# Compression pre-activations kept in PSUM, and softmax scales, minima and sums without two-tensor SBUF operations on VectorE

## The chip, the cores and the metric

The kernel runs on one core of a Trainium2 chip (trn2). The metric is the device time of one execution in microseconds (us); several runs are taken and their median is given. A profile of one execution gives, for every instruction of TensorE (PE, its weight loads PEld), VectorE (DVE), ScalarE (ACT), GpSimd (POOL) and of the DMA queues, when it started and how long it took.

## The reference, cut to what matters

One step of a decoder trunk: a prompt of 1024 tokens and eight single tokens, each with 8192 cached positions. The parts that the change touches are the compression of keys and values into blocks and the three softmax branches of the attention over the prompt:

```python
def compress(k, pe, w1, w2):                     # k: (B, T, G, 64)
    ...
    hid = pe.reshape(-1) @ w1                    # a bias
    for j in range(CMP_SEGS):                    # 2 segments of 16 positions
        hid = hid + jnp.einsum('bnsgd,sdh->bngh', seg[:, j:j + nc], w1r[j])
    return jax.nn.silu(hid) @ w2

def nsa_attend(...):
    s_c = jnp.einsum('bqgrd,bcgd->bgrqc', q, kc) + bias_c
    p_c = jax.nn.softmax(jnp.where(valid_c, s_c, NEG), axis=-1) * valid_c
    ...                                          # the same for selected blocks (p_s) and the window (p_w)
    g = jax.nn.sigmoid(gates)
    o = g[..., 0:1] * o_c + g[..., 1:2] * o_s + g[..., 2:3] * o_w
```

`compress` runs over the prompt's new rows and over the 8 x 8192 cached rows of keys and of values. All data are float32.

## The kernel before, in words

The program has three stages. The first (to about 440 us) projects the prompt and does the retention heads. The middle stage weaves two streams together: `attention()` over the prompt, and `compression()` of the caches with the decode attention behind it. The last stage does the output projection, the feed-forward network and the gated embedding.

`weave` takes generators that yield estimated costs and always advances the one with the smallest sum. It fixes the order in which instructions are issued, and a tile layer moves them a little against each other on each engine's queue. Every engine then works through its own queue in order and waits on semaphores.

**Attention** goes over 32 units (a 128-row tile of queries, a key group, a pair of heads; class `Unit`). Each has three branches: compressed (0), selected (1), window (2). For a branch, TensorE makes negated scores in PSUM banks `s`. VectorE adds the bias there and takes the minimum, `nmx`; where the scores have two pieces, the minimum of the second comes into a one-element tile `m2` and is joined to the first (L1080, helper line L139). ACT makes the exponentials into `pcm`, `psel` or `pwin` in SBUF with their sums in `sm` (L1094). Two partial sums are added (L1097, helper line L148). Then `scale` takes the reciprocal (L1046), multiplies it by the gate `gsig` (L1047, helper line L145) and multiplies the branch's tile by the product `scl`: on POOL for branches 0 and 2 (L1056), on ACT for branch 1 (L1052), as `ON = "GAG"` says. Last, `values` transposes the tiles on TensorE (L1141), ACT copies and rounds them (`ph`, L1146), VectorE takes the rest (`pl`, L142), and TensorE multiplies with the values (L1130, L1132).

**Compression** goes over 32 blocks (16 of keys, then 16 of values; a block is half of one sequence's cache). POOL gathers its pages by indirect DMA (L939), VectorE transposes them into `seg` tiles (L947), and the difference of two of them is taken half on VectorE and half on POOL (`differ`, L142). TensorE runs three passes of 8 matmuls (each stands twice in the trace, L918) into a PSUM bank `m`, of which there are two: with the weights of the second segment, then, on the block before, with the difference of the weights (`w1l` in the rows), then with those of the first segment. The hidden values are gated by silu as (tanh(x/2) + 1) * x/2:

```python
V.scalar_tensor_tensor(x, ph[:, :256], w[3][:, 0:1], d..., op0=ALU.add, op1=ALU.add)   # L1000
A.activation(t, x, AF.Tanh, scale=0.5)                                                # L1002
gated(pd, t, x, xhid[n][:, :, 128:256])                                               # L820
```

That is one half of a block's columns. The other half follows a block later in `hidden_act` (L826, L828), after the second pass has added to the same columns of the bank. In both, `x` (tile `ch_x`) and `t` (tile `ch_t`) are in SBUF, and `gated` (L820) makes the product `xh` from them on VectorE. A bank goes to the block after next once all that read it are done. `bank(...)` tiles are in PSUM, `tl(...)` tiles in SBUF. `prompt_blocks` uses `hidden_act` twice for the prompt's own rows.

Helpers record under one line whoever calls them: L139 any operation, L142 subtract, L145 multiply, L148 add.

Of the kernel before, what the change touches and what calls it, by code (L numbers as in the profile page):

```python
# [14 lines left out]
AF = mybir.ActivationFunctionType  # L15
ALU = mybir.AluOpType
AX = mybir.AxisListType.X
# [19 lines left out]
W_ATT, W_ATT2, W_DEC, W_VAL, W_RET, W_SP, W_T, ON, ORD = 1.6, 1.8, 0.5, 1.0, 3.0, (9000.0, 0.0, 6000.0, 0.0), (4000.0, 9000.0), "GAG", (0,7,1,6,2,5,3,4)  # L37
# [83 lines left out]
def hybrid_kernel(tc, I, C, O):  # L121
    nc = tc.nc
    V, G, A, P, SY = nc.vector, nc.gpsimd, nc.scalar, nc.tensor, nc.sync
# [6 lines left out]
    def tl(pool, shape, tag, dt=F32, bufs=None):  # L130
        kw = {} if bufs is None else {"bufs": bufs}
        return pool.tile(shape, dt, tag=tag, name=nm(tag), **kw)
# [5 lines left out]
    def tt(eng, out, a, b, op):  # L138
        eng.tensor_tensor(out=out, in0=a, in1=b, op=op)  # L139
# [4 lines left out]
    def mul(eng, out, a, b):  # L144
        eng.tensor_tensor(out=out, in0=a, in1=b, op=ALU.mult)  # L145

    def add(eng, out, a, b):
        eng.tensor_tensor(out=out, in0=a, in1=b, op=ALU.add)  # L148
# [34 lines left out]
    gsig = tl(pcd, [128, 9, 24], "gsig")  # L183
# [490 lines left out]
    for pair in range(2):  # L674
        rqk = tl(pr, [128, 2, 2, T], "rqk", bufs=1)
        rgs = tl(pr, [128, 2, T], "rgs", bufs=1)
        if pair:
# [3 lines left out]
            for t in range(9):  # L681
                pt, r = tok_major(wts, 256, t)
# [136 lines left out]
    def gated(p, t, x, dst):  # L819
        V.scalar_tensor_tensor(dst, t.rearrange("p (g n) -> p g n", g=2), 1.0, x.rearrange("p (g n) -> p g n", g=2),  # L820
                               op0=ALU.add, op1=ALU.mult)

    def hidden_act(p, w, ph, n, dst):

        t = tl(p, [128, 2 * n], "ch_t", bufs=2)
        A.activation(t[:, :2 * n], ph[:, :2 * n], AF.Tanh, bias=w[3][:, 1:2], scale=0.5)  # L826
        x = tl(p, [128, 2 * n], "ch_x", bufs=2)
        A.activation(x[:, :2 * n], ph[:, :2 * n], AF.Identity, bias=w[3][:, 0:1])  # L828
        gated(p, t[:, :2 * n], x[:, :2 * n], dst)


    def prompt_blocks():
# [121 lines left out]
    def compress_halves(n0, n1, w, tail, lag):  # L954

        done = n0
        phs, odd = {}, {}

        def parts(n, which):
            return seg[n, which, 0], seg[n, which, 1]  # L960

        for n in range(n0, n1 + 1):
            if n < n1:
                _, b, h = HALVES[n]
                ph = phs[n] = bank("m", 2)
                for k, _ in enumerate(half_mm(ph, w[1], parts(n, 0), True)):
                    if k in (0, 3):
                        turn_segments(n, 1, k // 3)
                    if k in (2, 5):
                        differ(n, k // 5)  # L970
                    if k in (6, 7):
                        fetch(n + 1, 1, [2 * k - 12, 2 * k - 11])
                    yield 430.0

                a = firsts[n] = tl(pd, [128, 2, 129], "first", bufs=2)
                A.copy(a[:, :, 0:128], ph[:, :256].rearrange("p (g n) -> p g n", g=2))
                if h:
                    G.memset(a[:, :, 128:129], 0.0)
                else:
                    G.tensor_copy(a[:, :, 128:129], firsts[n - 1][:, :, 0:1])  # L980
                d = tl(pd, [128, 2, 128], "follow", bufs=2)
                sub(G, d, a[:, :, 1:129], a[:, :, 0:128])
            if n > n0:
                m = n - 1
                for _ in half_mm(phs[m], w[4], parts(m, 2), False):
                    yield 430.0
                hidden_act(pd, w, phs[m], 128, xhid[m][:, :, 0:128])
            if n < n1:
                for k, _ in enumerate(half_mm(ph, w[0], parts(n, 1), False)):
                    if k in (0, 3):  # L990
                        turn_segments(n + 1, 0, k // 3)
                    if k in (5, 6):
                        fetch(n + 2, 0, [2 * k - 10, 2 * k - 9])
                    if k == 3 and done <= n - (1 if "ready" in E else lag):
                        yield from tail(done)
                        done += 1
                    yield 430.0
                xhid[n] = tl(pd, [128, 2, 256], "xh", bufs=4)
                x = tl(pd, [128, 256], "ch_x", bufs=2)
                V.scalar_tensor_tensor(x, ph[:, :256], w[3][:, 0:1], d.rearrange("p g n -> p (g n)"), op0=ALU.add, op1=ALU.add)  # L1000
                t = tl(pd, [128, 256], "ch_t", bufs=2)
                A.activation(t, x, AF.Tanh, scale=0.5)  # L1002
                gated(pd, t, x, xhid[n][:, :, 128:256])
                if "ready" in E and done <= n - 2:
                    yield from tail(done)
                    done += 1
        yield 1500.0
        for n in range(done, n1):
            yield from tail(n)
# [19 lines left out]
    class Unit:  # L1029
# [14 lines left out]
        def scale(u, br, dst, width, nmx, sm):  # L1044
            scl = tl(pp, [128, 2], "scl", bufs=4)
            V.reciprocal(scl, sm)  # L1046
            mul(V, scl, scl, gsig[:, u.i, br * 8 + u.h0:br * 8 + u.h0 + 2])  # L1047
            if u.i == 0 and br == 0:
                mul(V, scl, scl, rowv.to_broadcast([128, 2]))
            for r in range(2):  # L1050
                if ON[br] == "A":
                    A.mul(dst[:, r, :width], dst[:, r, :width], scl[:, r:r + 1])  # L1052
                elif ON[br] == "V":
                    V.tensor_scalar(dst[:, r, :width], dst[:, r, :width], scl[:, r:r + 1], None, op0=ALU.mult)
                else:
                    G.tensor_scalar(dst[:, r, :width], dst[:, r, :width], scl[:, r:r + 1], 1.0, op0=ALU.mult, op1=ALU.mult)  # L1056

        def branch(u, br, pieces, kind, dst, base_):
            nmx = tl(pp, [128, 2], "nmx", bufs=4)
            sm = tl(pp, [128, 2, 2], "sm", bufs=4)  # L1060
            for r in range(2):
                banks = []
                for x, (k0, n) in enumerate(pieces):
# [12 lines left out]
                    if lo < hi:  # L1076
                        if got:
                            m2 = tl(pp, [128, 1], "m2", bufs=4)
                            V.tensor_reduce(out=m2, in_=b[:, lo:hi], op=ALU.min, axis=AX)
                            tt(V, mn, mn, m2, ALU.min)  # L1080
                        else:
                            V.tensor_reduce(out=mn, in_=b[:, lo:hi], op=ALU.min, axis=AX)
                        got = True
# [9 lines left out]
                for x, (k0, n) in enumerate(pieces):  # L1093
                    A.activation(dst[:, r, (k0 - base_) * 128:(k0 - base_ + n) * 128], banks[x][:, :n * 128], AF.Exp,  # L1094
                                 bias=nmx[:, r:r + 1], scale=-1.0, accum_out=sm[:, r, x:x + 1])
            if len(pieces) == 2:
                add(V, sm[:, :, 0], sm[:, :, 0], sm[:, :, 1])  # L1097
            u.scale(br, dst, pieces[-1][0] * 128 + pieces[-1][1] * 128 - base_ * 128, nmx, sm[:, :, 0])

        def near_scores(u):  # L1100
            wc, nc0 = u.wc, max(0, u.wc - 15)
# [982 lines left out]
```

## Time and profile before

| | |
|---|---|
| median of 3 runs | 2201.52 us (2194.11 to 2202.75) |
| the profiled execution | 2201.91 us, its span 2200.1 us |
| mean granted TensorE clock | 0.977 of full speed |
| busy: PE, PEld | 2074.9 us (94%), 1912.1 us (87%) |
| busy: DVE, ACT, POOL | 1420.3 us (65%), 834.0 us (38%), 677.9 us (31%) |

The span runs from the first to the last instruction of the profiled execution. Matmuls are pipelined and the ends of their bars are modelled, so a busy PE is not a PE at its peak. A row of a group gives its busy time, the mean of one instruction, and the idle time of the engine just before them with what ended it. A row of a timeline gives start and duration; what stands in brackets is the idle time of the engine before it and its releaser.

### The profile page before, as it was taken

Reading aid. Unit: us, or ns where it says so; the run is one execution under the profiler, and the core shown is the slowest. Engines: PE = TensorE matmul, PEld = TensorE weight load, DVE = VectorE, ACT = ScalarE, POOL = GpSimd, SP = SyncE. Lnnn points to the kernel's source line nnn. Section 1 sums busy time; section 2 is a strip of 40 time slices with the busy share of each in tenths; the row PEclk is TensorE's granted clock in tenths of the full one; section 3 lists DMA queues with packets and bytes.
Section 4 is the critical chain, followed back from the end, with each engine's and each line's share of the span. In section 5 each row is a group of like instructions: output and inputs, shape, how many; then the busy total and the mean of one; then the engine's idle time right before and its main releaser. Section 6 shows DMA issues by size and latency. Waiting matters only on the chain. (4 is left out here: it accounts for less than half of the span.)

```text
span 2200.1 us, 38626 instructions
## 1 busy us (share of the span) xinstructions
PE 2074.9 (94%) x14856; PEld 1912.1 (87%) x14856; DVE 1420.3 (65%) x3231; ACT 834.0 (38%) x2027; POOL 677.9 (31%) x891
## 2 busy tenths in 40 slices
PE   7999999979899898899999899999999999999998
PEld 6998998867677776667999899999999999999998
DVE  4335245357788888768677437866766677878632
ACT  3331222235454454444444433332332334533321
POOL 1234334276666665656665023000000000000100
PEclk9999999979999999999999999999999999999999
DMA  6312213244333334443553442223223325644321
GB/s 220 126 58 70 68 51 83 61 131 122 100 107 106 96 106 123 151 147 119 164 156 114 125 148 78 73 92 112 97 92 109 103 92 176 193 118 144 92 78 49
DMA packets 183696, 244.65 MB, mean 111 GB/s; under 512 B 16980, under 2 KB 152808, under 8 KB 183320
## 3 DMA queue, kind: packets, MB, share of 16 engines
q1 hardware_dynamic: 158424, 158.28, 23.5%
q0 software_dynamic: 25088, 83.90, 12.4%
q8 instruction: 117, 1.92, 0.4%
q14 instruction: 67, 0.55, 0.1%
HBM read 201.99 MB, written 44.32 MB: 112 GB/s over the span
## 5 line engine op out<-in xcount | busy, mean ns | idle before, releaser
L918 PE MATMUL m<-seg,w1h 128*128 128x256 f32 x1024 | 302.9, 402 | 0.6 <-issue 0.6
L157 PE MATMUL s<-x,wu 128*128 128x258 f32 x872 | 249.4, 286 | 4.0 <-ACT x L152 1.4
L158 PE MATMUL s<-x,wu 128*128 128x258 f32 x872 | 248.6, 285 | 0.7 <-DVE x L142 0.7
L159 PE MATMUL s<-x,wu 128*128 128x258 f32 x872 | 247.9, 284 | 0.5 <-DVE wu L142 0.5
L157 PE MATMUL m<-x,wu 128*128 128x258 f32 x768 | 219.9, 287 | 3.7 <-DVE h L148 1.7
L158 PE MATMUL m<-x,wu 128*128 128x258 f32 x768 | 218.5, 285 | 2.5 <-DVE x L142 2.5
L159 PE MATMUL m<-x,wu 128*128 128x258 f32 x768 | 218.5, 285 | 0.0
L142 POOL TENSOR_TENSOR x<-h,x 128x516 fp32r<-128x516 f32 x4 | 5.6, 1412 | 677.4 <-ACT x L152 677.4
L918 PEld LDWEIGHTS m<-seg,w1h 128*128 128x128 f32 x1024 | 176.0, 197 | 19.8 <-issue 8.8
L947 DVE STREAM_TRANSPOSE seg<-raw 128x1024 f32<-128x1024 f32 x128 | 158.4, 1238 | 37.9 <-PE m L918 21.5
L152 ACT CAST wu<-wu 128x512 fp32r<-128x512 f32 (+2 forms) x178 | 109.6, 626 | 190.7 <-DVE wu L142 115.6
L157 PEld LDWEIGHTS s<-x,wu 128*128 128x128 f32 x872 | 166.0, 191 | 5.2 <-ACT x L152 1.9
L158 PEld LDWEIGHTS s<-x,wu 128*128 128x128 f32 x872 | 166.7, 191 | 1.3 <-DVE x L142 1.2
L159 PEld LDWEIGHTS s<-x,wu 128*128 128x128 f32 x872 | 166.4, 191 | 0.7 <-DVE wu L142 0.7
L142 DVE TENSOR_TENSOR wu<-wu,wu 128x512 fp32r<-128x512 f32 (+2 forms) x178 | 125.3, 707 | 59.6 <-ACT wu L152 57.9
L157 PE MATMUL t<-x,wu 128*128 128x258 f32 x528 | 151.2, 286 | 4.8 <-DVE h L148 1.9
L285 PE MATMUL g<-wh,xnh 128*128 128x256 f32 (+3 forms) x504 | 149.8, 298 | 2.3 <-ACT xnh L335 2.1
L157 PEld LDWEIGHTS m<-x,wu 128*128 128x128 f32 x768 | 146.6, 191 | 5.7 <-issue 1.7
L158 PE MATMUL t<-x,wu 128*128 128x258 f32 x528 | 150.0, 284 | 0.9 <-DVE x L142 0.9
L159 PE MATMUL t<-x,wu 128*128 128x258 f32 x528 | 149.7, 284 | 0.3 <-DVE wu L142 0.3
L158 PEld LDWEIGHTS m<-x,wu 128*128 128x128 f32 x768 | 147.1, 192 | 2.7 <-DVE x L142 2.7
L159 PEld LDWEIGHTS m<-x,wu 128*128 128x128 f32 x768 | 146.7, 191 | 0.0
(476 smaller groups left out, 6028.9 us busy)
## 6 DMA issues: line engine op xcount, KB each, us to landing
act_d<-act SPq DMA_DIRECT2D x22, 903.0 KB
wr<-in_w_in_dram SPq DMA_DIRECT2D x12, 1024.0 KB
wu<-in_w_gate_dram SPq DMA_DIRECT2D x22, 512.0 KB
wu<-in_w_up_dram SPq DMA_DIRECT2D x22, 512.0 KB
st<-act_d SPq DMA_DIRECT2D x42, 258.0 KB
wu<-in_w_down_dram SPq DMA_DIRECT2D x16, 512.0 KB
wst<-act_d SPq DMA_DIRECT2D x28, 258.0 KB
mr<-mix_d SPq DMA_DIRECT2D x16, 258.0 KB
```

What stands on the lines that cost most here:

```text
L142: eng.tensor_tensor(out=out, in0=a, in1=b, op=ALU.subtract)
L152: A.copy(hi, src)
L157: P.matmul(out, wh, xh, start=first, stop=False, **kw)
L158: P.matmul(out, wh, xl, start=False, stop=False, **kw)
L159: P.matmul(out, wl, xh, start=False, stop=last, **kw)
L285: P.matmul(pt[:r, :n], xh, wh[:, k, :n], start=k == 0, stop=False)
L918: P.matmul(out, w[:, k, :], x[:, k // 2 % 2, :, k % 2, :], start=first and k == 0, stop=k == 7, skip_group_check=not first)
L947: V.transpose(t.rearrange("p k (x d) -> p k x d", x=4), raws[n, par][:, :, s2 * 256:(s2 + 1) * 256].rearrange("p x (k d) -> p k x d", k=8))
```

## The change

Five edits, all around softmax and gating:

1. `hidden_act`: `x` is no longer a tile in SBUF but the bank's own columns; the Identity with the bias writes them in place.
2. `compress_halves`: `x` is the upper half of the bank (`ph[:, 256:512]`); the sum is written there and Tanh and `gated` read it there.
3. `scale`: the reciprocal is no longer multiplied by the gate on VectorE. POOL takes both factors as per-partition scalars of one instruction; for branch 1, ACT multiplies the reciprocal by the gate first, one column at a time.
4. `branch`, minima: the join of two minima takes one tensor and a per-partition scalar in place of two tensors.
5. `branch`, sums: a reduction over the pair in place of an addition of its two halves, into a tile of its own.

```diff
--- before.py
+++ after.py
@@ -823,10 +823,10 @@
     def hidden_act(p, w, ph, n, dst):
 
         t = tl(p, [128, 2 * n], "ch_t", bufs=2)
-        A.activation(t[:, :2 * n], ph[:, :2 * n], AF.Tanh, bias=w[3][:, 1:2], scale=0.5)
-        x = tl(p, [128, 2 * n], "ch_x", bufs=2)
-        A.activation(x[:, :2 * n], ph[:, :2 * n], AF.Identity, bias=w[3][:, 0:1])
-        gated(p, t[:, :2 * n], x[:, :2 * n], dst)
+        x = ph[:, :2 * n]
+        A.activation(t, x, AF.Tanh, bias=w[3][:, 1:2], scale=0.5)
+        A.activation(x, x, AF.Identity, bias=w[3][:, 0:1])
+        gated(p, t, x, dst)
 
 
     def prompt_blocks():
@@ -996,7 +996,7 @@
                         done += 1
                     yield 430.0
                 xhid[n] = tl(pd, [128, 2, 256], "xh", bufs=4)
-                x = tl(pd, [128, 256], "ch_x", bufs=2)
+                x = ph[:, 256:512]
                 V.scalar_tensor_tensor(x, ph[:, :256], w[3][:, 0:1], d.rearrange("p g n -> p (g n)"), op0=ALU.add, op1=ALU.add)
                 t = tl(pd, [128, 256], "ch_t", bufs=2)
                 A.activation(t, x, AF.Tanh, scale=0.5)
@@ -1044,16 +1044,15 @@
         def scale(u, br, dst, width, nmx, sm):
             scl = tl(pp, [128, 2], "scl", bufs=4)
             V.reciprocal(scl, sm)
-            mul(V, scl, scl, gsig[:, u.i, br * 8 + u.h0:br * 8 + u.h0 + 2])
+            gate = [gsig[:, u.i, br * 8 + u.h0 + r:br * 8 + u.h0 + r + 1] for r in range(2)]
             if u.i == 0 and br == 0:
                 mul(V, scl, scl, rowv.to_broadcast([128, 2]))
             for r in range(2):
                 if ON[br] == "A":
+                    A.mul(scl[:, r:r + 1], scl[:, r:r + 1], gate[r])
                     A.mul(dst[:, r, :width], dst[:, r, :width], scl[:, r:r + 1])
-                elif ON[br] == "V":
-                    V.tensor_scalar(dst[:, r, :width], dst[:, r, :width], scl[:, r:r + 1], None, op0=ALU.mult)
                 else:
-                    G.tensor_scalar(dst[:, r, :width], dst[:, r, :width], scl[:, r:r + 1], 1.0, op0=ALU.mult, op1=ALU.mult)
+                    G.tensor_scalar(dst[:, r, :width], dst[:, r, :width], scl[:, r:r + 1], gate[r], op0=ALU.mult, op1=ALU.mult)
 
         def branch(u, br, pieces, kind, dst, base_):
             nmx = tl(pp, [128, 2], "nmx", bufs=4)
@@ -1077,7 +1076,7 @@
                         if got:
                             m2 = tl(pp, [128, 1], "m2", bufs=4)
                             V.tensor_reduce(out=m2, in_=b[:, lo:hi], op=ALU.min, axis=AX)
-                            tt(V, mn, mn, m2, ALU.min)
+                            V.tensor_scalar(mn, m2, mn, None, op0=ALU.min)
                         else:
                             V.tensor_reduce(out=mn, in_=b[:, lo:hi], op=ALU.min, axis=AX)
                         got = True
@@ -1093,9 +1092,11 @@
                 for x, (k0, n) in enumerate(pieces):
                     A.activation(dst[:, r, (k0 - base_) * 128:(k0 - base_ + n) * 128], banks[x][:, :n * 128], AF.Exp,
                                  bias=nmx[:, r:r + 1], scale=-1.0, accum_out=sm[:, r, x:x + 1])
+            s = sm[:, :, 0]
             if len(pieces) == 2:
-                add(V, sm[:, :, 0], sm[:, :, 0], sm[:, :, 1])
-            u.scale(br, dst, pieces[-1][0] * 128 + pieces[-1][1] * 128 - base_ * 128, nmx, sm[:, :, 0])
+                s = tl(pp, [128, 2], "sm2", bufs=4)
+                V.reduce_sum(s, sm, axis=AX)
+            u.scale(br, dst, pieces[-1][0] * 128 + pieces[-1][1] * 128 - base_ * 128, nmx, s)
 
         def near_scores(u):
             wc, nc0 = u.wc, max(0, u.wc - 15)
```

The tile layer places instructions by its own estimates, so the queues were compared too. In VectorE's queue, in the key half of the compression, this is the place of one long `xh` product (`xh` gated hidden values, `nmx` minima, `sm` sums, `mo` an attention output, `scl` scales, `seg` transposed cache rows). Before:

```order
L142 TENSOR_TENSOR pl_6547<-t_6543,ph_6546 128x256
L820 SCALAR_TENSOR_TENSOR xh_6554<-ch_t_6557,ch_x_6555 128x2x128
L1082 TENSOR_REDUCE nmx_6573<-s_6575 128x1
L148 TENSOR_TENSOR sm_6502<-sm_6502 128x2
L148 TENSOR_TENSOR mo_6568<-o_6448,ot_6566 64x128
L1046 RECIPROCAL scl_6535<-sm_6502 128x2
L148 TENSOR_TENSOR mo_6568<-o_6448,ot_6566 64x128
L145 TENSOR_TENSOR scl_6535<-scl_6535,gsig_75 128x2
L1079 TENSOR_REDUCE m_1265_6586<-s_6583 128x1
L947 STREAM_TRANSPOSE seg_6684<-raw_6525 128x1024
L139 TENSOR_TENSOR nmx_6573<-nmx_6573,m_1265_6586 128x1
```

The same place of the same queue with the change:

```order
L142 TENSOR_TENSOR pl_6533<-t_6529,ph_6532 128x256
L820 SCALAR_TENSOR_TENSOR xh_6540<-ch_t_6542,m_6301 128x2x128
L1081 TENSOR_REDUCE nmx_6558<-s_6560 128x1
L1098 TENSOR_REDUCE sm_1241_6520<-sm_6488 128x2
L148 TENSOR_TENSOR mo_6553<-o_6436,ot_6551 64x128
L1046 RECIPROCAL scl_6522<-sm_1241_6520 128x2
L148 TENSOR_TENSOR mo_6553<-o_6436,ot_6551 64x128
L1078 TENSOR_REDUCE m_1259_6571<-s_6568 128x1
L947 STREAM_TRANSPOSE seg_6670<-raw_6511 128x1024
L1079 TENSOR_SCALAR nmx_6558<-m_1259_6571,nmx_6558 128x1
```

The list is the same but for the product with `gsig`, which is gone, and the operands: `xh` reads the bank `m`, the sum is a reduction, the minimum has one tensor input.

In ACT's queue, this is the scaling of one unit's selected branch (`psel`) with what stands around it (`pcm`, `pwin` the next unit's other branches, `ph` the copies that TensorE's value products read). Before:

```order
L1094 ACTIVATE psel_6169,sm_6171<-s_6194,nmx_6170 128x512
L1146 CAST ph_6262<-t_6257 128x512
L1002 ACTIVATE ch_t_6310<-ch_x_6308 128x256
L1052 ACTIVATE psel_6169<-psel_6169,scl_6213 128x1024 x2
L1115 ACTIVATE pcm_6287,sm_6296<-s_6290,nmx_6295 128x7 x2
```

With the change:

```order
L1093 ACTIVATE psel_6158,sm_6160<-s_6183,nmx_6159 128x512
L1002 ACTIVATE ch_t_6298<-m_6059 128x256
L1052 ACTIVATE scl_6202<-scl_6202,gsig_75 128x1 x2
L1053 ACTIVATE psel_6158<-psel_6158,scl_6202 128x1024 x2
L1116 ACTIVATE pcm_6277,sm_6286<-s_6280,nmx_6285 128x7 x2
```

Two instructions of one element per partition stand ahead of the two scalings; one `ph` copy moved to another place.

## Rows read from the trace of the kernel before

**Rows 1.** The page, its first part: busy time of an engine in us, its share of the span, and its instructions.

```profile
PE 2074.9 (94%) x14856; PEld 1912.1 (87%) x14856; DVE 1420.3 (65%) x3231; ACT 834.0 (38%) x2027; POOL 677.9 (31%) x891
```

**Rows 2.** Busy time by stretch, middle stage. Columns: the stretch and its length in us; busy us and instructions of PE, PEld, DVE, ACT, POOL; granted clock; share of the DMA engines; GB/s.

```profile
460.00:560.00 100.00, 88.83 (x455) 71.74 (x456) 76.11 (x193) 47.08 (x146) 70.99 (x89) 0.92 0.41 122
560.00:660.00 100.00, 91.64 (x511) 74.26 (x510) 79.24 (x196) 55.08 (x156) 66.11 (x81) 0.97 0.35 105
660.00:760.00 100.00, 89.93 (x496) 73.45 (x494) 81.46 (x182) 48.19 (x142) 68.27 (x80) 0.95 0.35 105
760.00:860.00 100.00, 90.75 (x509) 73.01 (x510) 88.81 (x197) 51.58 (x144) 54.76 (x69) 0.98 0.35 104
860.00:1000.00 140.00, 127.04 (x728) 91.29 (x728) 97.18 (x277) 63.09 (x159) 83.16 (x96) 0.95 0.48 150
1000.00:1240.00 240.00, 237.87 (x1538) 214.19 (x1537) 169.30 (x402) 102.73 (x277) 138.88 (x160) 1.00 0.41 124
```

**Rows 3.** Groups of VectorE's instructions by line and shape: first 460 to 1000 us (four rows), then 1000 to 1240 us (two rows). Busy us and mean ns of one stand behind the bar.

```profile
L820 DVE SCALAR_TENSOR_TENSOR xh<-ch_t,ch_x 128x256 f32<-128x256 f32 x41 | 36.6, 892 | 1.6 <-ACT ch_x L828 0.9 <-ACT ch_t L1002 0.5
L145 DVE TENSOR_TENSOR scl<-scl,gsig 128x2 f32<-128x2 f32 x71 | 23.0, 325 | 0.9
L139 DVE TENSOR_TENSOR nmx<-nmx,m 128x1 f32<-128x1 f32 x23 | 7.9, 341 | 0.2
L148 DVE TENSOR_TENSOR sm<-sm 128x2 f32<-128x2 f32 x23 | 5.6, 243 | 1.5 <-ACT psel L1094 0.5 <-issue 0.4 <-ACT pwin L1094 0.3
...
L820 DVE SCALAR_TENSOR_TENSOR xh<-ch_t,ch_x 128x256 f32<-128x256 f32 x22 | 14.9, 679 | 1.1 <-ACT ch_t L1002 1.0
L145 DVE TENSOR_TENSOR scl<-scl,gsig 128x2 f32<-128x2 f32 x25 | 7.9, 314 | 0.4
```

**Rows 4.** Groups of VectorE's instructions over the whole span: neighbours in size or kind.

```profile
L1046 DVE RECIPROCAL scl<-sm 128x2 f32<-128x2 f32 x96 | 14.5, 152 | 5.7 <-ACT pwin L1094 1.8 <-ACT pcm L1115 1.2 <-issue 1.2
L1000 DVE SCALAR_TENSOR_TENSOR ch_x<-m,bb,follow 128x256 f32<-128x256 f32 x32 | 15.4, 481 | 11.2 <-PE m L918 5.7 <-issue 2.2 <-PE t L1141 1.6
L1448 DVE TENSOR_SCALAR s<-s 64x1 f32<-64x1 f32 x2 | 0.3, 146 | 0.1
L1113 DVE TENSOR_REDUCE nmx<-s 128x2 f32<-128x14 f32 x4 | 0.7, 164 | 0.1
```

**Rows 5.** The timeline of one long `xh` product and of an undisturbed one: start us, duration us, engine, line.

```profile
599.35 1.02 POOL L939 DMA_INDIRECT raw<-in_cache_cmp_k_dram,cix  x1 [0.17 <-issue]
599.71 3.37 DVE L820 SCALAR_TENSOR_TENSOR xh<-ch_t,ch_x 128x256 f32<-128x256 f32 x1
600.39 2.39 POOL L142 TENSOR_TENSOR seg<-seg,seg 128x1024 f32<-128x1024 f32 x1
604.36 0.16 DVE L145 TENSOR_TENSOR scl<-scl,gsig 128x2 f32<-128x2 f32 x1
605.54 0.33 PE L1141 MATMUL t<-c_ident,pwin 128*128 128x128 f32 x1 [1.55 <-POOL pwin L1056]
606.32 0.48 PE L1141 MATMUL t<-c_ident,pwin 128*128 128x128 f32 x1 [0.44 <-POOL pwin L1056]
606.58 1.91 PE L918 MATMUL m<-seg,w1l 128*128 128x256 f32 x4
...
617.33 0.42 DVE L820 SCALAR_TENSOR_TENSOR xh<-ch_t,ch_x 128x256 f32<-128x256 f32 x1 [0.94 <-ACT ch_x L828]
```

**Rows 6.** Three more long products and TensorE's idle time behind each, from the timelines of 552 to 562, 665 to 674 and 802 to 812 us (VectorE and TensorE).

```profile
552.23 2.50 DVE L820 SCALAR_TENSOR_TENSOR xh<-ch_t,ch_x 128x256 f32<-128x256 f32 x1
555.80 0.45 PE L1066 MATMUL s<-kst,qa 128*128 128x384 f32 x1 [1.55 <-ACT pcm L1115]
...
665.08 3.17 DVE L820 SCALAR_TENSOR_TENSOR xh<-ch_t,ch_x 128x256 f32<-128x256 f32 x1 [0.48 <-ACT ch_t L1002]
670.65 0.39 PE L1130 MATMUL o<-ph,cvst 128*128 128x256 f32 x1 [2.70 <-ACT ph L1146]
...
802.35 3.12 DVE L820 SCALAR_TENSOR_TENSOR xh<-ch_t,ch_x 128x256 f32<-128x256 f32 x1
806.13 0.39 PE L1132 MATMUL o<-pl,vst 128*128 128x256 f32 x1 [2.25 <-DVE pl L142]
```

**Rows 7.** TensorE's waits from 460 to 1000 us, three of them: who waited for whom, us in total, times, the longest.

```profile
PE o L1132 <- DVE pl L142: 10.1, 9, 2.3
PE t L1141 <- POOL pwin L1056: 9.8, 10, 2.0
...
PE t L1141 <- ACT psel L1052: 3.2, 2, 3.0
```

**Rows 8.** Groups of ACT's instructions and one of POOL's, over the middle stage or the whole span: prices that the change is costed by.

```profile
L828 ACT ACTIVATE ch_x<-m,bb 128x256 f32<-128x256 f32 x32 | 15.2, 475 | 0.0
L1002 ACT ACTIVATE ch_t<-ch_x 128x256 f32<-128x256 f32 x32 | 13.4, 419 | 10.7 <-DVE ch_x L1000 8.5 <-issue 1.4 <-DVE s L148 0.6
L1453 ACT ACTIVATE pnew<-snew,s 64x1 f32<-64x1 f32 x2 | 0.6, 294 | 1.8 <-DVE s L1448 1.8
L745 ACT ACTIVATE bb<-r 128x1 f32<-128x1 f32 x2 | 0.4, 178 | 0.0
L1056 POOL TENSOR_SCALAR pcm<-pcm,scl 128x128 f32<-128x128 f32 x64 | 26.3, 421 | 26.9 <-DVE scl L145 17.1 <-DVE cand L1348 4.1 <-DVE s L148 3.6
```

## The prediction

> **What bounds the kernel now.** The page comes first [rows 1]: TensorE is busy 94% of the span and VectorE 65%, but the mean hides stages with other limits. So I read the busy time by stretch of the middle stage, where attention and the compression of the cache run woven together and where every edit but two instructions lies [rows 2]. From 460 to 1000 us TensorE is busy for 88.83 + 91.64 + 89.93 + 90.75 + 127.04 = 488.2 of 540 us, so 51.8 us are idle, at a granted clock of 0.92 to 0.98. From 1000 to 1240 us it is busy for 237.87 of 240 us at 1.00. Only the first part has time to win. There VectorE is busy for 76.11 + 79.24 + 81.46 + 88.81 + 97.18 = 422.8 us, 78%: too full to run far ahead, and TensorE waits for what stands behind it.
>
> The groups by shape come next [rows 3]. Four kinds of VectorE instruction take far longer than their size. The gating product `xh<-ch_t,ch_x` means 892 ns before 1000 us; at 617.33, undisturbed, it took 0.42 us [rows 5]. `scl<-scl,gsig`, of two elements, means 325 ns against 0.16 in an undisturbed case [rows 5]; `nmx<-nmx,m` means 341 and `sm<-sm` 243. All four read two tensors in SBUF. Neighbours of the same sizes with one such operand do not show it: the reciprocal of two elements means 152 ns over 96, and the PSUM-reading `ch_x<-m,bb,follow` means 481 over 32 [rows 4].
>
> The timeline shows why [rows 5]. The product that starts at 599.71 runs 3.37 us; a gather runs on POOL from 599.35, the POOL difference `seg` from 600.39 for 2.39 us, and the product ends 0.3 us after that one. Behind it VectorE is late with the sum, the reciprocal and the product for `scl` at 604.36; TensorE's transposes of `pwin`, which POOL scales by it, wait 1.55 and 0.44 us. Three more long products look alike, with TensorE idle 1.55, 2.70 and 2.25 us shortly after [rows 6]. The waits of TensorE up to 1000 us [rows 7] are led by two such ends, `pl` from VectorE (10.1 us) and `pwin` from POOL (9.8 us).
>
> **The change, part by part.** VectorE before 1000 us, delay first [rows 3]: the gating product 36.6 - 41 x 0.42 = 19.4 us; `scl` 23.0 - 71 x 0.16 = 11.6; `nmx` 7.9 - 23 x 0.16 = 4.2; `sm` 5.6 - 23 x 0.16 = 1.9. Together 37.1 us of delay that goes if delay needs two SBUF inputs.
>
> The plain cost changes less. The 71 `scl` products vanish: 71 x 0.16 = 11.4 us. The gating product now reads x from PSUM; its price is bounded by 0.42 and by the 481 ns of the instruction nearest to it, of the same operation and 256 elements with a PSUM input and a scalar operand [rows 4]. I take 0.48, so 41 x 0.06 = 2.5 us come back. The minimum becomes a one-input instruction, near a 64x1 one of 146 ns; the sum becomes a reduction, near 164 ns for 14 elements [rows 4]: no change from 0.16. VectorE is relieved of 37.1 + 11.4 - 2.5 = 46.0 us before 1000 us, and after it of 14.9 - 22 x 0.48 = 4.3, plus 7.9 for `scl`: 12.2 us.
>
> [...] The new minimum is a single-input fp32 `tensor_scalar` in SBUF; the row that stands for it is undelayed at 146 ns, but that is two instructions only [rows 4]. [...]
>
> How much reaches the end? The ends are nothing, if TensorE's idle time has other causes, and all 51.8 us. The four episodes [rows 5, 6] lie between and are the nearest rows: delays of 2.95, 2.08, 2.75 and 2.70 us, 10.5 in all, were followed by 1.99 + 1.55 + 2.70 + 2.25 = 8.5 us of idle TensorE, 0.81 of it. But TensorE idles 9.6% of this part anyway; over some 28 us around the episodes that is 2.7 us, which leaves 0.55. I take 0.7 of the delay: 26 us. The plain relief of 8.9 us is spread thinly and mostly fills VectorE's own idle time: 0.2 of it, 2 us. After 1000 us TensorE has 2.1 us of idle time: 1 us.
>
> ACT gets 64 instructions of one element per partition, two ahead of each scaling of `psel`. Bounds are 178 ns (a PSUM source) and 294 ns [rows 8]; 0.25 x 64 = 16 us, some three quarters of them before 1000 us, where ACT is busy 265 of 540 us [rows 2]. `psel` is consumed a unit later, behind the near values and the next near scores, which hides them. What ACT has queued behind them is the copy `ph`, for which TensorE waits: I charge 2 us, and up to 12 if that cover fails. The Tanh reads PSUM instead of SBUF: at most the 475 ns of the PSUM-reading Identity for 419, 32 x 0.056 = 2 us on ACT [rows 8]. The Identity writes PSUM in place and the first gating sum likewise, at unshown prices; their present 475 [rows 8] and 481 [rows 4] are the nearest, with no sign either way, and I take no change. POOL's 128 scalings read a second per-partition scalar for an immediate; today 421 ns at 128 elements [rows 8]. I take no change, since they also lose one step of waiting: they hang on the reciprocal now, no longer on the product. The two prompt compressions before 460 us are worth nothing.
>
> The order of issue hardly moves: around the long product VectorE's queue is the same list less the product for `scl`, and ACT's the same with the two new rows. SP's and POOL's queues keep their work.
>
> **Sum.** 26 + 2 + 1 - 2 = 27 us. The profiled execution took 2201.9 us, its span 2200.1, and the median of the runs is 2201.5, so both agree: **2175 us**. A higher clock is left to the range: it stands below 1.00 wherever TensorE idles [rows 2].
>
> **Rivals.** *The relief is absorbed.* TensorE's gaps in this part come from the loops of scores, exponentials and transposes; then the four VectorE steps shorten and its idle time grows by the same 40 us or so. For it: `psel` from ACT stands among the releasers too [rows 7], and VectorE is idle for 540 - 422.8 = 117 us of this part [rows 2]. Against it: the episodes. Time 2192 to 2204.
>
> *POOL becomes dearer.* If the second scalar operand adds X to each of 128 scalings, `pwin` and `pcm` reach TensorE 2X later per branch. About three quarters of the 32 units lie before 1000 us; 24 x 4X eats the gain of 27 at X = 0.28 us, and at X = 0.5 us the time is 2175 + 48 = 2223. Against it: the form with one scalar operand and an immediate costs 421 ns in all, waiting included [rows 8], and X would have to be two thirds of that.
>
> *The bank is held.* x now lives in the PSUM bank that collects the compression: in its upper half for the first gating product of a block, in its lower half, in place, for the second. The first product must end before the bank's next matmuls, those with `w1l`; the second before the bank goes to the block after next, a whole pass of matmuls later. In the long episode the product ended at 603.08 and the first `w1l` matmul started at 606.58 [rows 5], so 3.5 us were spare. If that cover goes and each of some 30 blocks waits 1.5 us, the time is 2175 + 45 = 2220. [...]
>
> **How the numbers follow.** Forecast 0.72, absorbed 0.16, POOL 0.07, bank 0.05. A measurement here can tell about 0.5%, 11 us. Faster takes 0.70 of the forecast; its last 0.02, the absorbed case and 0.02 of the bank are no change, 0.20; the rest is slower, 0.10. The low end is all 51.8 us of idle time, 2150. The high end is no gain and some cost on ACT, 2205; only the two slower cases and an unforeseen gain in clock lie outside.
>
> **What would show it.** Right: L820 near 0.45 us with no long ones, no VectorE `scl` product but the four with `rowv`, TensorE's idle time from 460 us to the old 1000 us mark halved, the end of the middle stage some 25 us earlier, and the stages after it as long as now. Wrong: L820 still at 0.8 us (the delay does not need two SBUF inputs), the same idle time behind other releasers (absorbed), L1056 above 0.6 us at 128 elements (POOL), or TensorE's L918 waiting for L820 (bank).

## The result and the profile after

The changed kernel takes 2166.23 us (median of 4 runs, 2158.61 to 2169.09) against 2198.89 us for the kernel before (4 runs with the ones shown above): ratio 0.9848, 95% interval 0.9822 to 0.9874. It is 33 us faster; the forecast was 2175 us, some 27 us faster, with a range of 2150 to 2205. The profiled execution took 2167.84 us, its span 2166.1 us.

The page's first part, to be set against [rows 1]: VectorE is busy 50 us less, TensorE 10 us less, POOL and ACT 10 us more each.

```profile
PE 2064.8 (95%) x14856; PEld 1906.0 (88%) x14856; DVE 1370.6 (63%) x3135; ACT 844.3 (39%) x2091; POOL 688.4 (32%) x891
```

To see where the 34 us of span went, both spans are cut at the same places of TensorE's program: the first matmul of the compression, the first of its block 22 (the two stretches in between hold the same 2762 matmuls), the last gating product, the end. The views are busy time by stretch, columns as in [rows 2]. Before:

```profile
0.00:460.10 460.10, 424.89 (x3124) 401.65 (x3124) 190.56 (x523) 132.03 (x331) 152.03 (x274) 0.98 0.30 94
460.10:1011.30 551.20, 499.48 (x2762) 392.10 (x2763) 431.65 (x1061) 271.67 (x759) 349.02 (x419) 0.95 0.40 120
1011.30:1240.80 229.50, 226.57 (x1469) 205.83 (x1467) 160.76 (x381) 96.88 (x264) 133.05 (x153) 1.00 0.40 122
1240.80:2200.10 959.30, 923.99 (x7504) 912.50 (x7504) 637.34 (x1268) 333.44 (x674) 43.77 (x46) 0.98 0.36 112
```

After:

```profile
0.00:465.70 465.70, 431.55 (x3123) 407.36 (x3123) 190.81 (x523) 132.58 (x331) 152.02 (x274) 0.96 0.30 93
465.70:979.70 514.00, 484.16 (x2762) 381.55 (x2763) 393.90 (x989) 279.06 (x807) 357.08 (x419) 0.98 0.41 129
979.70:1211.50 231.80, 228.09 (x1469) 207.40 (x1467) 148.51 (x357) 99.49 (x280) 135.39 (x153) 0.99 0.39 121
1211.50:2166.10 954.60, 920.99 (x7504) 909.66 (x7504) 637.40 (x1268) 333.19 (x674) 43.93 (x46) 0.99 0.36 112
```

All of the gain lies in the second stretch: 551.2 to 514.0 us, 37.2 less. TensorE's idle time there falls from 551.2 - 499.5 = 51.7 to 514.0 - 484.2 = 29.8 us, 21.9 less. The other 15.3 us are busy time, for the same number of matmuls: the granted clock was 0.95 and is 0.98. The other three stretches give +5.6, +2.3 and -4.7 us; in the first and the last too the granted clock moved with the length.

VectorE's groups from 460 to 1000 us, the counterparts of [rows 3] (`L820`, `L1079` for `nmx`, `L1098` for `sm`; the product for `scl` is gone) and of the PSUM-reading sum in [rows 4]:

```profile
L820 DVE SCALAR_TENSOR_TENSOR xh<-ch_t,m 128x256 f32<-128x256 f32 x44 | 17.9, 408 | 2.7 <-PE s L1266 1.4 <-issue 0.6 <-ACT ch_t L1002 0.5
...
L1000 DVE SCALAR_TENSOR_TENSOR m<-m,bb,follow 128x256 f32<-128x256 f32 x23 | 11.2, 488 | 6.5 <-PE m L918 2.9 <-POOL pcm L1055 1.1 <-issue 1.0
...
L1079 DVE TENSOR_SCALAR nmx<-m,nmx 128x1 f32<-128x1 f32 x24 | 4.8, 202 | 0.3
...
L1098 DVE TENSOR_REDUCE sm<-sm 128x2 f32<-128x4 f32 x24 | 3.3, 139 | 2.8 <-ACT psel L1093 1.7 <-ACT pwin L1093 0.7 <-issue 0.4
```

The gating product means 408 ns for 892. No instance of it, of the minimum or of the sum is long any more: in the whole middle stage the longest took 0.42, 0.22 and 0.16 us.

ACT's groups from 460 to 1240 us, the counterparts of two of [rows 8] and the new products:

```profile
L1052 ACT ACTIVATE scl<-scl,gsig 128x1 f32<-128x1 f32 x64 | 15.5, 292 | 4.5 <-DVE scl L1046 3.7 <-issue 0.8
L828 ACT ACTIVATE m<-m,bb 128x256 f32<-128x256 f32 x32 | 14.4, 448 | 0.0
L1002 ACT ACTIVATE ch_t<-m 128x256 f32<-128x256 f32 x32 | 12.3, 385 | 10.9 <-DVE m L1000 7.1 <-DVE s L148 2.1 <-issue 1.6
```

POOL's scaling, over the same stretch:

```profile
L1055 POOL TENSOR_SCALAR pcm<-pcm,scl,gsig 128x128 f32<-128x128 f32 x64 | 30.9, 488 | 9.0 <-DVE scl L1046 8.1
```

TensorE's waits from 460 to 1000 us, against [rows 7]:

```profile
PE t L1142 <- POOL pwin L1055: 7.1, 7, 2.4
PE t L1142 <- issue: 3.7, 3, 3.0
...
PE o L1133 <- DVE pl L142: 2.1, 6, 0.6
...
PE t L1142 <- DVE pl L142: 1.0, 2, 0.6
```

The wait for `pl`, which VectorE makes, falls from 10.1 to 2.1 us and its longest from 2.3 to 0.6; that for `pwin` only from 9.8 to 7.1. The three waits under `issue` are for the scaled `psel`, as their rows in the timeline show.

### The profile page after: what moved, and what is told of

Its sections match the earlier page's. It is cut to its first block, busy times and chain, and to the rows that moved or that the text cites. A ratio compares the mean times of both kernels' runs of the same rounds, so it can differ in the third digit from the quotient of the medians.

```text
span 2166.1 us, 38533 instructions
## 1 busy us (share of the span) xinstructions
PE 2064.8 (95%) x14856; PEld 1906.0 (88%) x14856; DVE 1370.6 (63%) x3135; ACT 844.3 (39%) x2091; POOL 688.4 (32%) x891
## 3 DMA queue, kind: packets, MB, share of 16 engines
q0 software_dynamic: 25088, 83.90, 12.3%
## 5 line engine op out<-in xcount | busy, mean ns | idle before, releaser
L918 PE MATMUL m<-seg,w1h 128*128 128x256 f32 x1024 | 297.7, 397 | 0.9 <-DVE seg L947 0.5
L918 PEld LDWEIGHTS m<-seg,w1h 128*128 128x128 f32 x1024 | 173.7, 194 | 20.9 <-issue 9.1
L947 DVE STREAM_TRANSPOSE seg<-raw 128x1024 f32<-128x1024 f32 x128 | 158.6, 1240 | 42.0 <-PE m L918 26.0
L157 PEld LDWEIGHTS m<-x,wu 128*128 128x128 f32 x768 | 145.6, 190 | 5.7 <-issue 2.4
L158 PEld LDWEIGHTS m<-x,wu 128*128 128x128 f32 x768 | 146.2, 190 | 2.7 <-DVE x L142 2.7
L286 PE MATMUL g<-wl,xnh 128*128 128x256 f32 (+3 forms) x504 | 147.3, 292 | 0.4 <-DVE wl L142 0.4
```

What stands on the lines that cost most here:

```text
L157: P.matmul(out, wh, xh, start=first, stop=False, **kw)
L158: P.matmul(out, wh, xl, start=False, stop=False, **kw)
L286: P.matmul(pt[:r, :n], xh, wl[:, k, :n], start=False, stop=False)
L918: P.matmul(out, w[:, k, :], x[:, k // 2 % 2, :, k % 2, :], start=first and k == 0, stop=k == 7, skip_group_check=not first)
L947: V.transpose(t.rearrange("p k (x d) -> p k x d", x=4), raws[n, par][:, :, s2 * 256:(s2 + 1) * 256].rearrange("p x (k d) -> p k x d", k=8))
```

## Experiments

Theory: the gain is the delay that VectorE's instructions with two SBUF tensors suffer while POOL works (the delay theory). Rivals: the product for `scl` left the way from the reciprocal to POOL's scaling (the chain theory); or a gain of the clock that needs most of the idle time to go at once (the clock theory).

The table sums them up. "Delay" is the busy time, in the middle stage, of those of the kinds in question (`xh`, `scl`, `nmx`, `sm`) that still read two tensors in SBUF, or of the added instruction, less their count times the plain 0.415, 0.16, 0.158 and 0.147 us. "Idle" and "busy" are TensorE's in the stretch that answers to the second one above, from one profiled execution each. Ratios are to the kernel before, run beside each kernel.

| kernel | ratio (95%) | delay us | idle us | busy us |
|---|---|---|---|---|
| before | 1 | 49 | 51.7 | 499.5 |
| the change | 0.9848 (0.9822 to 0.9874) | 0 | 29.8 | 484.2 |
| x_psum | 0.9920 (0.9892 to 0.9948) | 26 | 33.4 | 483.0 |
| scale_only | 0.9947 (0.9917 to 0.9977) | 43 | 41.0 | 486.2 |
| minsum_only | 0.9970 (0.9944 to 0.9995) | 47 | 40.7 | 489.8 |
| extra_two | 0.9916 (0.9889 to 0.9942) | 26 | 41.3 | 486.4 |
| extra_one | 0.9914 (0.9883 to 0.9946) | 29 | 42.4 | 485.7 |
| extra_recip | 0.9838 (0.9811 to 0.9866) | 0 | 31.2 | 485.9 |
| extra_odd | 0.9847 (0.9820 to 0.9874) | 0 | 29.8 | 490.5 |
| pool_one_input | 0.9877 (0.9837 to 0.9916) | 35 | 30.6 | 481.8 |
| pool_one_late | 0.9863 (0.9831 to 0.9896) | 32 | 39.9 | 485.8 |
| before_split | 1.0006 (0.9979 to 1.0033) | 49 | 56.5 | 492.7 |
| after_split | 0.9828 (0.9795 to 0.9860) | 0 | 28.6 | 482.6 |
| one_scalar | 0.9821 (0.9793 to 0.9848) | 0 | 29.9 | 486.1 |

### The edits apart: x_psum, scale_only, minsum_only

Edits 1 and 2, edit 3, and edits 4 and 5 of the diff above, each alone on the kernel before.

> Edits 1 and 2 alone (x in PSUM). Delay theory (the gain comes from VectorE instructions that wait for POOL because they read two SBUF tensors, in proportion to their delay: gating product 25.8 of 52.7 us in the middle stage): L820 at 0.41 us with none above 0.5, the delays of scl, sm and nmx as before (some 27 us), time about 16 us below before, 2183. Chain theory (the gain comes from the product with the gate that left the way from reciprocal to POOL's scaling): within 5 us of before, 2194 or more. Clock theory (the gain needs TensorE's idle time to fall far enough that the clock stays up): at most half of 16 us, 2191 or more, with as many stretches at the low clock as before.

> Edit 3 alone (both factors on POOL, the gate on ACT for branch 1). Delay theory: 17.2 of 52.7 us of delay and 11 us of plain product go, POOL's scalings cost 0.076 us more: about 11 us below before, 2188. L820 still means about 0.8 us. Chain theory: the larger part of the whole gain, 20 us or more, 2179 or less. Clock theory: 5 us or less, 2194 or more.

> Edits 4 and 5 alone (minimum with a scalar operand, sum as a reduction). Delay theory: 9.7 of 52.7 us of delay go: about 6 us below before, 2193, minima near 0.20 us and sums near 0.14 us, none long. Chain theory and clock theory: no change, within 3 us of 2199. If a one-input instruction in SBUF waited for POOL too, L1079 would keep means near 0.3 us.

Measured beside a median of 2191.20 us: 2173.63, 2181.68 and 2184.43, by the ratios 17.5, 11.6 and 6.6 us less. The delay theory had 16, 11 and 6. Each of the three has an interval of some 6 us to either side. They add up to 35.7 us where the whole change gives 33: no threshold shows, so the clock theory falls, and the chain theory as the whole cause falls with the first of them.

VectorE's groups over the middle stage, with x in PSUM alone:

```profile
L145 DVE TENSOR_TENSOR scl<-scl,gsig 128x2 f32<-128x2 f32 x96 | 33.3, 348 | 1.2
L820 DVE SCALAR_TENSOR_TENSOR xh<-ch_t,m 128x256 f32<-128x256 f32 x64 | 26.3, 411 | 7.3 <-ACT m L828 5.3 <-ACT ch_t L1002 1.8
```

With the new scales alone:

```profile
L820 DVE SCALAR_TENSOR_TENSOR xh<-ch_t,ch_x 128x256 f32<-128x256 f32 x64 | 61.7, 964 | 6.0 <-ACT ch_x L828 4.2 <-ACT ch_t L1002 1.7
```

With the new minima and sums alone:

```profile
L820 DVE SCALAR_TENSOR_TENSOR xh<-ch_t,ch_x 128x256 f32<-128x256 f32 x64 | 57.1, 892 | 5.8 <-ACT ch_x L828 4.3 <-ACT ch_t L1002 1.4
...
L1080 DVE TENSOR_SCALAR nmx<-m,nmx 128x1 f32<-128x1 f32 x32 | 6.4, 201 | 0.3
```

Only the edited kinds lose their delay. One thing was not expected: where the gating product keeps x in SBUF, its own mean rises (811 ns over this stage before, 964 and 892 here). The relief of one kind went partly into the waits of another, so the sums of delay in these profiles fall by less (49 to 43 and 47) than the removed kinds had. The times came as the delay theory forecast, but the net delay fell by 23, 6 and 2 us for 17.5, 11.6 and 6.6 us of time. With one profile each, a gain in proportion to the delay isn't shown.

### An instruction that nobody reads: extra_two, extra_one, extra_recip, extra_odd

Each adds one line to `scale` of the changed kernel, behind the reciprocal, 96 times in all (`spare`, and one of the four lines under it):

```diff
+            spare = tl(pp, [128, 2], "spare", bufs=4)
+            mul(V, spare, scl, gsig[:, u.i, br * 8 + u.h0:br * 8 + u.h0 + 2])       # extra_two
+            V.tensor_scalar(spare, scl, 1.0, None, op0=ALU.mult)                    # extra_one
+            V.reciprocal(spare, scl)                                                # extra_recip
+            V.tensor_scalar(spare, scl[:, 0:1], 1.0, None, op0=ALU.mult)            # extra_odd, spare [128, 1]
```

> The changed kernel with the product of reciprocal and gate put back on VectorE at its old place (two elements, two SBUF tensors, 96 times), but into a tile that nobody reads: no instruction waits for its result, only VectorE's queue does. Delay theory: it takes 0.16 us plain and 0.3 us on average, 14 to 19 us of delay and 15 us plain; the time rises by 8 to 14 us over the change, to 2174 to 2180. Chain theory (the product only cost because POOL waited for it): within 3 us of the change.

> The same with one SBUF tensor instead of two (the reciprocal times the constant 1.0 into a tile that nobody reads, 96 times). Delay theory: 0.12 to 0.18 us each, none long; the time within 4 us of the change, 8 us or so below the variant with two tensors. Rival (any further VectorE instruction costs as much): as slow as the variant with two tensors.

> The changed kernel with a further reciprocal of two elements behind the first, into a tile that nobody reads, 96 times. A reciprocal never showed a delay (152 ns, at most 193). Delay theory: some 0.15 us each, 15 us of plain work and no delay: the time within 4 us of the change, ratio to before 0.985 to 0.987, 10 us below the two variants whose extra instruction waits 27 to 30 us. Rival (any extra instruction at this place costs 15 us, whether it waits or not): ratio 0.991 to 0.992.

> The changed kernel with a tensor_scalar with one SBUF tensor, as in the variant with one tensor, but of one element per partition instead of two, into a tile that nobody reads, 96 times. If the wait for POOL comes with an even count of elements: 0.13 to 0.2 us each, none above 0.25, ratio to before 0.985 to 0.987. If every tensor_scalar in SBUF waits: a mean of 0.45 us as with two elements, some 28 us of delay, ratio 0.991 to 0.992.

Over the middle stage the added instruction took, in this order:

```profile
L145 DVE TENSOR_TENSOR spare<-scl,gsig 128x2 f32<-128x2 f32 x96 | 40.9, 427 | 1.2
```
```profile
L1051 DVE TENSOR_SCALAR spare<-scl 128x2 f32<-128x2 f32 x96 | 44.7, 467 | 1.2
```
```profile
L1051 DVE RECIPROCAL spare<-scl 128x2 f32<-128x2 f32 x96 | 14.9, 156 | 1.2
```
```profile
L1051 DVE TENSOR_SCALAR spare<-scl 128x1 f32<-128x1 f32 x96 | 13.7, 144 | 1.1
```

The expectation for extra_one was wrong: with one SBUF tensor and two elements the instruction waits as the one with two tensors does, 467 ns on average. With one element it doesn't. The times follow the waits, not the count of instructions: 0.9914 and 0.9916 with 26 to 29 us of delay, 0.9838 and 0.9847, the change's own ratio, with 14 to 15 us of undelayed work. So some 27 us of delay cost about 0.0068 x 2200 = 15 us, and 96 undelayed instructions in the same place cost nothing beyond the intervals, some 6 us to either side. That doesn't make delay dearer than other work, since rows of VectorE overlap in part. Its busy time, which counts an overlap once, is 542.4 us in the middle stage of the changed kernel (393.90 + 148.51 above), 572.0 and 573.1 with extra_two and extra_one, 544.8 with extra_recip and 548.7 with extra_odd. The delayed instruction adds 30 us to it and costs 15, the undelayed one adds 2 to 6; at the same rate that would cost 1 to 3 us, too little to be seen here.

How it reaches TensorE, in the timeline of extra_one (start us, duration us):

```profile
765.32 2.67 DVE L1051 TENSOR_SCALAR spare<-scl 128x2 f32<-128x2 f32 x1
765.34 2.37 POOL L142 TENSOR_TENSOR seg<-seg,seg 128x1024 f32<-128x1024 f32 x1
...
767.89 0.41 DVE L820 SCALAR_TENSOR_TENSOR xh<-ch_t,m 128x256 f32<-128x256 f32 x1
...
768.51 1.27 DVE L142 TENSOR_TENSOR pl<-t,ph 128x512 fp32r<-128x512 f32 x2
...
769.24 0.39 PE L1135 MATMUL o<-pl,vst 128*128 128x256 f32 x1 [1.66 <-DVE pl L142]
```

Two elements take 2.67 us and end at 767.99, as POOL's difference ends at 767.71. Behind them `pl` is late, and TensorE stands for 1.66 us. Over the stretch to 1000 us, TensorE's waits for `pl`, with extra_one:

```profile
PE o L1135 <- DVE pl L142: 10.0, 8, 2.5
```

and with extra_odd:

```profile
PE o L1135 <- DVE pl L142: 2.2, 4, 0.7
```

One limit: in the selected branch ACT multiplies `scl` in place and must wait until the added instruction has read it. ACT's idle time before those products that ends with `spare` was 17.5 us with extra_one, so the 15 us need not have gone through VectorE's queue alone.

### POOL's side: pool_one_input, pool_one_late, before_split, after_split

The first two replace POOL's difference in the kernel before by two instructions with one SBUF tensor, which leaves out the subtraction for half of the columns; the second of them reads `seg[n, 1, s2]`:

```diff
-        sub(G if s2 else V, t, seg[n, 0, s2], seg[n, 1, s2])
+        if s2:
+            for _ in range(2):
+                G.tensor_scalar(t, seg[n, 0, s2], 1.0, 1.0, op0=ALU.mult, op1=ALU.mult)
+        else:
+            sub(V, t, seg[n, 0, s2], seg[n, 1, s2])
```

The other two cut the difference in two, in the kernel before and in the changed one:

```diff
-    def differ(n, s2):
-        t = seg[n, 2, s2] = tl(pd, [128, 8, 128], "seg", bufs=8)
-        sub(G if s2 else V, t, seg[n, 0, s2], seg[n, 1, s2])
+    def differ(n, k):                                  # called at k = 2, 4 and 5
+        s2 = int(k > 2)
+        ...                                            # the tile is made at k = 2 and 4
+        h = slice(0, 8) if k == 2 else slice(0, 4) if k == 4 else slice(4, 8)
+        sub(G if s2 else V, seg[n, 2, s2][:, h, :], seg[n, 0, s2][:, h, :], seg[n, 1, s2][:, h, :])
```

> The kernel before, none of the five edits, but POOL's difference of two seg tiles (two SBUF tensors, 2.37 us) is replaced by two one-input instructions of the same size on the first of them (the subtraction of this half of the columns is left out), so that POOL stays about as busy. Delay theory in its narrow form (the delay needs two SBUF tensors on VectorE and on POOL at once): L820 falls from a mean of 0.82 to below 0.55 us, scl to about 0.2, the sum of delays from 53 to below 15 us, and the time by 15 to 28 us, 2171 to 2184, with VectorE's program unchanged. Rival (any POOL instruction in SBUF delays them): delays stay at 40 us or more and the time within 6 us of before. Chain theory: delays fall but the time stays within 6 us.

> As the variant of the kernel before whose POOL difference became two one-input instructions, but they read the second of the two seg tiles, the later one, so that POOL cannot start them earlier than the difference (the subtraction of this half of the columns is left out). If that variant gained by shorter waits on VectorE: the sum of delays again near 37 us instead of 51 and the time 15 to 27 us below before. If it gained because POOL started earlier: delays near 37 us, the time 10 us or less below before. If the count of inputs on POOL does not matter: delays of 50 us and the time of before.

> The kernel before, none of the five edits, with POOL's difference of the seg tiles cut into two instructions of 512 columns in place of one of 1024, which stand behind each other in POOL's queue. If a delayed VectorE instruction gets through as soon as one POOL instruction ends: the longest delays fall from 3 us to some 1.5 us, the sum of delays from 51 to some 35 us and the time by 10 to 27 us, as with the one-input instructions. If it only gets through when POOL is idle or out of such work: delays and time as before, within 5 us. If the one-input variant gained because POOL's scalings came through earlier, the time stays too, since no scaling stands between the two halves.

> The changed kernel with the same cut. Delay theory: nothing left to shorten, within 4 us of the change (2162 to 2170), and a little POOL work added. If the cut helps by POOL's own queue (scalings, gathers), it gains here as much as in the kernel before, 10 us or more.

POOL's new instruction and two of VectorE's groups in pool_one_input, middle stage:

```profile
L954 POOL TENSOR_SCALAR seg<-seg 128x1024 f32<-128x1024 f32 x64 | 68.3, 1067 | 11.8 <-PE m L918 10.1
```
```profile
L820 DVE SCALAR_TENSOR_TENSOR xh<-ch_t,ch_x 128x256 f32<-128x256 f32 x64 | 40.6, 634 | 6.2 <-ACT ch_x L828 4.6 <-ACT ch_t L1006 1.4
L145 DVE TENSOR_TENSOR scl<-scl,gsig 128x2 f32<-128x2 f32 x96 | 24.0, 251 | 1.3
```

The narrow form of the theory is wrong: POOL's instructions with one SBUF tensor delay VectorE too. The delays fall from 49 to 35 us and not below 15; what is shorter is the single wait, since POOL's instruction takes 1.07 us for 2.37. Yet 25.4 of 2191.20 us were gained on the medians (2165.75), and 27.7 of 2204.57 with the later operand (2176.85), where POOL can't start earlier. So an early start of POOL is not the cause, and VectorE's program is the same as before: what POOL does meanwhile is enough to move the time by as much as most of the change. That 14 to 17 us less delay bring 25 us or more is more per us than x_psum and the added instructions show; POOL's instructions at this place were also shorter (68.3 us for 75.7), and this isn't separated.

The cut alone shows nothing. POOL's halves stand behind each other:

```profile
L142 POOL TENSOR_TENSOR seg<-seg,seg 128x512 f32<-128x512 f32 x64 | 80.4, 1279 | 14.8 <-DVE scl L145 6.2 <-PE m L918 3.4 <-PE s L1268 2.5
```

and VectorE's product waits as before:

```profile
L820 DVE SCALAR_TENSOR_TENSOR xh<-ch_t,ch_x 128x256 f32<-128x256 f32 x64 | 52.3, 816 | 6.6 <-ACT ch_x L828 4.9 <-ACT ch_t L1005 1.4
```

The expectation that a waiting instruction gets through as soon as one POOL instruction ends was wrong for two differences in a row: the halves leave no gap in POOL's queue, their rows overlap by some 0.04 us. The rows of the one-input instructions of pool_one_input don't overlap (64 x 1067 ns are their 68.3 us of busy time), and there the delays were shorter, 35 us for 49. That a gap decides isn't shown. In the changed kernel the cut gives 0.9828, inside the change's interval.

### The price of POOL's second scalar: one_scalar

The changed kernel without the gates of branches 0 and 2:

```diff
-                    G.tensor_scalar(dst[:, r, :width], dst[:, r, :width], scl[:, r:r + 1], gate[r], op0=ALU.mult, op1=ALU.mult)
+                    G.tensor_scalar(dst[:, r, :width], dst[:, r, :width], scl[:, r:r + 1], 1.0, op0=ALU.mult, op1=ALU.mult)
```

> The changed kernel with the constant 1.0 in place of the gate as POOL's second factor (the gates of the compressed and the window branch are left out): L1055 at 361 ns instead of 437 at 128 elements, 128 times 0.076 = 9.7 us less POOL work, of which 0.15 us per branch lie between reciprocal and transposes. If this price reaches TensorE in about the share in which VectorE's delay does: 2 to 6 us below the change; if POOL's scalings are covered: no change within 2 us.

```profile
L1055 POOL TENSOR_SCALAR pcm<-pcm,scl 128x128 f32<-128x128 f32 x64 | 25.0, 402 | 8.8 <-DVE scl L1046 8.0
```

402 ns for 488: the second scalar costs some 0.08 us. The ratio is 0.9821 for 0.9848, with intervals that overlap, and TensorE's idle time is the same (29.9 and 29.8 us): inconclusive, 6 us by the ratios and 0 by the idle time.

## Why the prediction held, and where it did not

**The bound.** Right: TensorE's idle time before 1000 us was where time could be won, and all of the gain lies there. After it TensorE had little to give; the third stretch is no shorter. Its sign, TensorE's idle time halved, was nearly met: 51.7 to 29.8 us.

**The delay.** Right, and shown: the four kinds lost it, L820 to 0.41 us. In the kernel before, 19 of their instances lost over 1 us each; 17 of these end within 0.35 us of the end of POOL's difference, the other two behind a scaling of `pwin`. The reason was stated too narrowly. "Two tensors in SBUF" is not the whole condition, since extra_one waits with one. For the minimum of edit 4, which has one element, the prediction took the row of the one-element instruction (146 ns, [rows 4]). The runs agree with that row: a `tensor_scalar` in SBUF means 467 ns with two elements (extra_one) and 144 with one (extra_odd), and none of the 32 minima took over 0.22 us. Why one element doesn't wait isn't shown, and no experiment tried a third count.

**How much reaches the end.** The total was near, 33 us for 27, but its main term is made of two. Of the 37.1 us of delay, 0.7 was to come out of idle time, 26 us. Measured in the equal stretch, idle time fell by 21.9 us, 0.59 of the delay; the net estimate of the prediction, 0.55, was nearer than the 0.7 it took. The rest goes with the granted clock, 0.95 to 0.98, worth 15.3 us of busy time for the same matmuls, which the prediction left to the range. So it is partly luck that the total came near: a share put too high stood in for a clock that wasn't in the sum. How much of that the change causes is not settled: busy time in this stretch is 482 to 491 us in all kernels with 29 to 42 us of idle time, and 499.5 and 492.7 in the two with over 50; one profile each does not fix it closer.

**The plain relief.** 2 us were taken for 8.9 us of plain work. Undelayed instructions of 14 to 15 us by their rows, put back, cost nothing beyond some 6 us to either side (extra_recip, extra_odd), which agrees with 2 us but can't fix it. The relief itself was over-counted: the sum by rows had 46.0 us before 1000 us, and VectorE's busy time in the second stretch fell by 431.65 - 393.90 = 37.8 us, since rows overlap; after it the fall was 12.3 us for 12.2.

**The prices of the PSUM forms.** The product was put at 0.48 and took 0.408, below even the undisturbed 0.42 [rows 5]; Tanh fell from 419 to 385 ns and the Identity from 475 to 448 ns [rows 8]. No cost came back.

**ACT.** 64 products at 292 ns, 0.25 was taken. Their cover held on the whole: TensorE's waits for the scaled `psel` were 3.2 us before [rows 7] and are 3.7 us after, where the profile puts them under `issue`. The long one is the same wait in both kernels, before and after:

```profile
502.63 0.33 PE L1141 MATMUL t<-c_ident,psel 128*128 128x128 f32 x1 [3.02 <-ACT psel L1052]
...
508.27 0.33 PE L1142 MATMUL t<-c_ident,psel 128*128 128x128 f32 x1 [3.04 <-issue]
```

**POOL dearer.** X was put at nothing and is 0.07 to 0.10 us (at 128 elements 488 ns for 421 before and for 402 in one_scalar, at 640 elements 974 for 875), far below the 0.28 at which that rival decides.

**The bank held.** Between 440 and 1240 us TensorE's L918 waited for L820 once, 0.6 us, at the `w1l` matmul of 1204.76. The wait exists; the spare time covers it.

**Outside the middle stage.** The first stretch is 5.6 us longer with a granted clock of 0.96 for 0.98. In the experiments on the changed kernel, where this stage is the same, it took from 456.4 to 461.8 us, so this is not the change. The last stretch was 954 to 961 us in all of them.

## What to carry to other kernels

Compare an instruction's mean with its undisturbed duration; where small VectorE instructions show means of twice that (here 892 ns for 420 and 325 for 160), look at what POOL was doing under the long ones, and price the delay, not the instruction. It can be removed without less work: one operand in PSUM (here 408 ns for 892), a reduction for a sum of two (139 for 243), a scalar operand on one element (202 for 341). A delay in an in-order queue costs those behind it: here 27 us of delay cost 15 us, and as many undelayed instructions, which add only 2 to 6 us to VectorE's busy time, nothing that could be measured.

## What the runs showed of the hardware beyond that

- A `tensor_scalar` on two fp32 elements in SBUF means 467 ns over 96, with one of 3.71 us (extra_one); on one element it means 144 ns over 96 (extra_odd).
- A reciprocal of two elements and a reduction of two pairs showed no wait for POOL: in the kernels before and after they took at most 0.19 and 0.16 us. In extra_one a reciprocal of 0.32 us stood behind a delayed instruction.
- POOL delays VectorE with one SBUF tensor as well as with two: 35 us of delay in pool_one_input, 49 in the kernel before. Two halves in a row hold VectorE as long as one whole does: the gating product means 816 ns in before_split and 811 before. In the single wait of extra_one at 765.32, VectorE's row ahead ran to 765.46, and POOL's difference started before that, at 765.34.
- In the kernel before, 59 instructions of the four kinds started under a POOL gather of the cache (L939) with no other POOL work beside it, and none lost more than 0.03 us. Where a two-tensor difference followed the gather at once, six of them lost 2.3 to 3.0 us, counted from within the gather, as the product at 599.71 [rows 5]. In three of these (599.71, 665.08, 729.83) VectorE's row starts 0.5 to 0.7 us ahead of the difference and is long all the same; why is open.
